# A hybrid encoder block on one core: the weight sums of a seven-product matrix multiply, made by loads, an accumulating DMA and VectorE instead of GpSimd

## The chip, the cores and the metric

The kernel runs on one core of a Trainium2 chip. The metric is the device time of one execution in microseconds. The engines are named as the profile names them: PE is TensorE (PEld its weight loads), DVE is VectorE, ACT is ScalarE, POOL is GpSimd, and SP is the engine whose queue carries most transfers.

## The reference, cut to what matters

The program is one encoder layer on 512 rows of 1024 values: three gated token mixers, an output projection, and a feed-forward block. The change lies in the feed-forward block:

```
x = x + merged @ w_out
h2 = rms_norm(x, g_ffn)                                  # 512 x 1024
ffn = (silu(h2 @ w_ffn_gate) * (h2 @ w_ffn_up)) @ w_ffn_down   # hidden width 2816
return rms_norm(x + ffn, g_final)
```

All values are float32.

## The kernel before, in words

**Precision.** Each float32 operand of a matrix product is split in two reduced parts, `hi` and `lo` (`split`, L85 on ACT makes hi by a copy, L86 on DVE makes lo by a subtraction; L88 and L89 do the same with a scale). A product is three matmuls a step: hi by hi (L104), hi by lo (L105) and lo by hi (L106). The profile cuts a tile's name at its last number, so the tiles `s34_hi`, `a22_lo` and `s12` of the code are `s_hi`, `a_lo` and `s` in its rows, `h2t3h` is the high part of t3, and `po` and `pg` are banks of PSUM.

**The feed-forward block.** The hidden width of 2816 is 22 tiles f of 128. Tiles 0 to 2 are made plainly (`ffn_plain`). Tiles 3 to 21 treat gate and up weights of one tile together as a 2 by 2 matrix of blocks: a holds the gate weights (a11 and a12, its two halves of 512), b the up weights (a21 and a22). With `h2` cut in four blocks they are done in seven block products instead of eight (`ffn_first`, `ffn_second`, `ffn_third`), in the manner of Strassen and Winograd. That takes four sums of weight blocks per tile (s1 to s4, in `lhs_side`) and four sums of blocks of h2, made once (t1 to t4, in `rhs_sums`). A product of a tile is 12 matmuls of 256 columns (4 blocks of 128 rows, three matmuls each), so seven products are 84.

**Loads and buffers.** SP's queue loads a into `raw` (two buffers, shared with all other weight loads) and b into `rawb` (two). POOL makes the four sums into `s12` (two buffers) and `s34r` (one). ACT and DVE split a, s12, s34r and half of b; the split of a and s12 goes to `w_hi` and `w_lo` (three buffers in turn).

**After the products.** ACT and DVE make the gated activation u of a tile. For f from 4 on it is stored to DRAM (L950, SP's queue) and loaded again (L1039) for the last product with `w_ffn_down` (`projection`, called a second time), because the tiles of that product lie where those of the seven products lay.

**Order.** A scheduler puts the instructions of each engine in an order when the program is built; on the chip each engine and each queue then works in that order. A tile's buffer is taken again when those that read it are done.

Of the kernel before, what the change touches and what calls it, by code (L numbers as in the profile page):

```python
# [11 lines left out]
F32 = mybir.dt.float32  # L12
# [3 lines left out]
ALU = mybir.AluOpType  # L16
# [3 lines left out]
P = 128  # L20
S = 512
# [39 lines left out]
def block_kernel(ctx, tc, x, mem, pos, inv, g_mix, mem_g, g_ffn, g_final, g_q, g_kv, gate_bias,  # L61
# [78 lines left out]

    def lhs_side(pool, srcs):
# [33 lines left out]
    with ExitStack() as mix:  # L175
# [684 lines left out]
        gfin_b = keep.tile([P, D], F32, name="gfin_b")  # L860
        bcast_rows(gfin_b, g_final)
# [30 lines left out]
        def projection(banks, w, nch, tail, lhs, hold, early, done, prep=None):  # L892
            vs = []
            for half in range(2):
# [11 lines left out]
                if half == 0:  # L906
                    for t in range(NT):
                        ss = keep.tile([P, 1], F32, name="ssx", tag="ssx", bufs=2 * NT)
                        add_part(parts[t][0][0], t, 0, H, ss)
                        vs.append(partial(ss, EPS))  # L910
                        early(t)
                else:
                    wcs = hold(lead)
                    for t in range(NT):
                        for part in parts[t]:
# [4 lines left out]
                            add_part(ps[:, :n], t, H + c0, n, ss)  # L920
# [14 lines left out]
        projection(((po,) * 4, (po,) * 3, (po, pg)), w_out, 4, 4, lambda c: (mg_hi, mg_lo, 2 * c), hold_out, lambda t: None, to_h2)  # L935
# [42 lines left out]
    def kept(src, name):  # L978
        t = fg.tile([P, HS], F32, name=name, tag=name, bufs=1)
# [3 lines left out]
    def ffn_first(f):  # L983
# [5 lines left out]
        g1 = fg.tile([P, HS], F32, name="g1", tag="g1", bufs=1)  # L989
# [54 lines left out]
    xg = [last.tile([P, D], F32, name=f"xg{t}") for t in range(NT)]  # L1044

# [6 lines left out]
    def store(t, r):  # L1052
# [4 lines left out]
        for c0 in range(H, D, n):  # L1057
# [5 lines left out]
               w_fd, NF // 2, 3, act_side, hold_down, gain_low, store, act_load)  # L1063
# [81 lines left out]
```

## Time and profile before

| | |
|---|---|
| median of 3 runs | 952.23 us (950.2 to 952.91) |
| the profiled execution: its time | 951.96 us |
| its span on the core | 949.0 us |
| busy: PE, DVE, ACT, POOL | 911.5, 649.7, 510.0, 213.7 us |
| tiles by seven products, even part of the stretch | 632.85 to 797.6 us |

The span is the time from the first to the last recorded instruction of the core; the execution's time holds the start and the end around it too. Busy time of an engine is the sum of its instructions; matmuls are pipelined, so a busy PE need not be at its peak. A wait is put down to what came last before the instruction started.

### The profile page before, as it was taken

What the parts mean: (1) busy time and instruction counts of PE and PEld (TensorE: products, weight loads), DVE (VectorE), ACT (ScalarE), POOL (GpSimd) and SP (SyncE); (2) the same over time, 40 slices, a digit from 0 to 9 for tenths busy, and PEclk for the clock granted to TensorE, in tenths of its full rate; (3) what the DMA queues carried; (4) which work ended last, traced back from release to release, by engine and by line L of the source; (5) the groups of instructions that cost most, each with busy time, mean ns of one, the idle gap of its engine ahead of it and who ended that gap; (6) DMA issues with size and microseconds to landing.
All of it is one profiled execution on the core that took longest, in us unless ns stands there. A gap on an engine that the chain in (4) does not pass through costs nothing.

```text
span 949.0 us, 14065 instructions
## 1 busy us (share of the span) xinstructions
PE 911.5 (96%) x5282; PEld 789.7 (83%) x5282; DVE 649.7 (68%) x1031; ACT 510.0 (54%) x896; POOL 213.7 (23%) x215
## 2 busy tenths in 40 slices
PE   7998999999999999999999999989999999799996
PEld 5987887788788788888888789889999999688885
DVE  5678968787766656775557568889888897362322
ACT  7566767776653556777663446444454454251222
POOL 2000002212112101010014100866656652000200
PEclk9999999999999999999999999999999999999999
DMA  7421244444322122112224521323333332382322
GB/s 268 155 73 52 90 138 134 137 134 139 130 93 92 42 89 70 62 51 83 89 79 166 176 69 59 142 99 120 127 112 112 114 134 79 128 268 89 102 76 89
DMA packets 37252, 105.88 MB, mean 112 GB/s; under 512 B 5233, under 2 KB 7601, under 8 KB 37185
## 3 DMA queue, kind: packets, MB, share of 16 engines
q1 hardware_dynamic: 35136, 100.69, 31.8%
q0 software_dynamic: 1184, 3.24, 1.0%
q10 hardware_dynamic: 864, 1.06, 0.3%
q8 instruction: 41, 0.67, 0.3%
q14 instruction: 27, 0.21, 0.1%
HBM read 98.08 MB, written 6.90 MB: 111 GB/s over the span
## 4 chain that ended last, share of the span: by engine, by line
PE 76%; DVE 8%; ACT 4%; DMA 4%; POOL 3%; issue 3%; POOLq 0%; SPq 0%; DVEq 0%; ACTq 0%
PE pg L104 15%; PE pg L105 15%; PE pg L106 15%; PE po L106 5%; PE po L104 5%; PE po L105 5%; DVE s_lo L86 3%; ACT s_hi L85 2%; PE psc L104 2%; PE psc L105 2%; PE psc L106 2%; PE ptp L815 1%; DMA e<-a_dr 1%; DVE w_lo L86 1%; DMA raw<-w_out_d 1%
## 5 line engine op out<-in xcount | busy, mean ns | idle before, releaser
L86 DVE TENSOR_TENSOR w_lo<-raw,w_hi 128x1024 fp32r<-128x1024 f32 (+3 forms) x131 | 151.1, 1155 | 108.8 <-ACT w_hi L85 106.1
L85 ACT ACTIVATE w_hi<-raw 128x1024 fp32r<-128x1024 f32 (+3 forms) x131 | 127.1, 972 | 142.8 <-PE pg L105 86.6
L104 PE MATMUL pg<-h_hi,w_hi 128*128 128x512 f32 (+1 forms) x476 | 175.2, 369 | 1.0 <-DVE q_lo L89 0.6
L105 PE MATMUL pg<-h_lo,w_hi 128*128 128x512 f32 (+1 forms) x476 | 175.6, 369 | 0.0
L106 PE MATMUL pg<-h_hi,w_lo 128*128 128x512 f32 (+1 forms) x476 | 175.1, 368 | 0.3 <-DVE w_lo L86 0.3
L104 PEld LDWEIGHTS pg<-h_hi,w_hi 128*128 128x128 f32 x476 | 89.6, 188 | 15.6 <-DVE q_lo L89 0.8
L106 PEld LDWEIGHTS pg<-h_hi,w_lo 128*128 128x128 f32 x476 | 89.4, 188 | 14.9 <-DVE w_lo L86 0.7
L105 PEld LDWEIGHTS pg<-h_lo,w_hi 128*128 128x128 f32 x476 | 89.5, 188 | 13.6
L571 POOL TENSOR_SCALAR_AFFINE_SELECT e<-e 128x128 f32<-128x128 f32 x64 | 24.6, 394 | 120.3 <-ACT e L568 112.9
L568 ACT ACTIVATE e<-e,ccol 128x512 f32<-128x512 f32 (+3 forms) x64 | 32.3, 554 | 28.7 <-DMA e<-a_dr 28.7
L85 ACT ACTIVATE s_hi<-s34r 128x1024 fp32r<-128x1024 f32 x19 | 20.2, 1061 | 51.3 <-PE pg L105 39.7
L150 POOL TENSOR_TENSOR s<-rawb 128x512 f32<-128x512 f32 x19 | 33.5, 1761 | 62.9 <-DMA rawb<-w_fu_d 62.9
L1070 DVE TENSOR_REDUCE nm<-psc 128x1 f32<-128x512 f32 (+1 forms) x48 | 27.7, 596 | 19.9 <-PE psc L106 19.5
L573 DVE TENSOR_TENSOR e<-e,psc 128x512 f32<-128x512 f32 (+3 forms) x64 | 29.1, 482 | 17.1 <-POOL e L571 15.5
L1073 ACT ACTIVATE pn<-psc,nm 128x512 f32<-128x512 f32 (+1 forms) x48 | 29.3, 613 | 17.7 <-DVE nm L1070 17.6
L86 DVE TENSOR_TENSOR s_lo<-s34r,s_hi 128x1024 fp32r<-128x1024 f32 x19 | 23.4, 1233 | 19.3 <-ACT s_hi L85 19.3
L104 PE MATMUL po<-w_hi,act_hi 128*128 128x512 f32 (+1 forms) x84 | 32.5, 387 | 3.4 <-ACT act_hi L88 3.4
L240 POOL TENSOR_TENSOR merged<-merged,th 128x512 f32<-128x512 f32 x8 | 11.8, 1476 | 104.5 <-DVE th L239 64.7
L86 DVE TENSOR_TENSOR w_lo<-s,w_hi 128x1024 fp32r<-128x1024 f32 x19 | 34.0, 1792 | 1.7 <-ACT w_hi L85 1.7
L153 POOL TENSOR_TENSOR s34r<-raw,s 128x512 f32<-128x512 f32 x19 | 34.7, 1826 | 0.0
L104 PE MATMUL po<-h_hi,w_hi 128*128 128x256 f32 (+1 forms) x116 | 33.7, 291 | 0.9 <-ACT w_hi L85 0.9
L106 PE MATMUL po<-h2t3h,s_lo 128*128 128x256 f32 x76 | 23.3, 306 | 11.8 <-DVE s_lo L86 11.8
(509 smaller groups left out, 2666.9 us busy)
## 6 DMA issues: line engine op xcount, KB each, us to landing
raw<-w_zt_d SPq DMA_DIRECT2D x46, 512.0 KB, 3.4
raw<-w_fg_d SPq DMA_DIRECT2D x22, 512.0 KB, 3.5
raw<-w_fd_d SPq DMA_DIRECT2D x22, 512.0 KB, 3.5
e<-a_dr SPq DMA_DIRECT2D x32, 320.0 KB, 3.5
rawb<-w_fu_d SPq DMA_DIRECT2D x19, 512.0 KB, 3.4
raw<-w_br_d SPq DMA_DIRECT2D x12, 512.0 KB, 3.4
act_dr<-u SPq DMA_DIRECT2D x18, 256.0 KB, 2.6
act<-act_dr SPq DMA_DIRECT2D x18, 256.0 KB, 3.9
```

The costliest lines, as they stand in the source:

```text
L85: A.activation(hi, src, AF.Copy)
L86: V.tensor_tensor(out=lo, in0=src, in1=hi, op=ALU.subtract)
L104: mm(ps, wh, ah, start=start and i == 0, stop=False, skip_group_check=more)
L105: mm(ps, wh, al, start=False, stop=False, skip_group_check=more)
L106: mm(ps, wl, ah, start=False, stop=stop and i == n - 1, skip_group_check=more)
L150: G(out=s12[:, u], in0=b[:, u], in1=b[:, v], op=ALU.add)
L153: G(out=s34[:, v], in0=a[:, v], in1=s12[:, v], op=ALU.subtract)
L568: A.activation(e[:, c0:c0 + n], e[:, c0:c0 + n], AF.Exp, bias=ccol[:, j, d, row:row + 1])
L571: nc.gpsimd.affine_select(out=dg, in_=dg, pattern=[[sgn, P]], compare_op=ALU.is_ge, fill=0.0, base=0, channel_multiplier=-sgn)
L573: V.tensor_tensor(out=e[:, c0:c0 + n], in0=e[:, c0:c0 + n], in1=sc[:, t0:t0 + n], op=ALU.mult)
L1070: nc.vector.tensor_reduce(out=nm, in_=sc, axis=AX.X, op=ALU.max, negate=True)
L1073: nc.scalar.activation(pn, sc, AF.Exp, bias=nm, accum_out=sm)
```

## The change

The sums are chosen so that all are plain additions, up to signs that are taken back elsewhere. s1 and s3 lie in one tile, s13: SP loads a22 into its first half and a11 into its second, and one DMA on POOL's queue, with the addition done by the DMA, adds a21 to both. s2 and s4 lie in s24 and are made by DVE from s13 and a: s2 is s1 + a11, s4 is s2 + a12. s13 and s24 have two buffers each. The tiles m1, g1, u2 and u4 have two instead of one. In `rhs_sums` the signs follow (two sums are now a negated sum in one three-operand instruction), and the activation of tiles from 3 on gets its sign back by a scale of -0.5. Room is found by moving tiles to other pools: the junk tile, the final gain `gfin_b` (whose load then comes later), and rt3; the reloaded `act` tiles move to a pool that exists before the seven products begin.

```diff
@@ rhs_sums
+        def put_neg(name, out, in0, in1):
+            V.scalar_tensor_tensor(out=out, in0=in0, scalar=-1.0, in1=in1, op0=ALU.mult, op1=ALU.subtract)
+            split(*dst[name], out)
+
         put("t3", pool.tile([P, KH, HS], F32, name="rt3"), b22, b12)
-        put("t1", b12, b12, b11)
-        put("t2", b22, b22, b12)
-        put("t4", b21, b21, b22)
+        put("t1", b12, b11, b12)
+        put_neg("t2", b22, b12, b22)
+        put_neg("t4", b21, b22, b21)
@@ lhs_side
-        for raw, src in zip((a, b), srcs):
-            nc.sync.dma_start(out=raw, in_=src)
+        s13, s24 = (pool.tile([P, 1024], F32, name=n, tag=n, bufs=2) for n in ("s13", "s24"))
         u, v = slice(0, 512), slice(512, 1024)
-        s12, s34 = (pool.tile([P, 1024], F32, name=n, tag=n, bufs=b) for n, b in (("s12", 2), ("s34r", 1)))
-        G = nc.gpsimd.tensor_tensor
-        G(out=s12[:, u], in0=b[:, u], in1=b[:, v], op=ALU.add)
-        G(out=s12[:, v], in0=s12[:, u], in1=a[:, u], op=ALU.subtract)
-        G(out=s34[:, u], in0=a[:, u], in1=b[:, u], op=ALU.subtract)
-        G(out=s34[:, v], in0=a[:, v], in1=s12[:, v], op=ALU.subtract)
+        sa, sb = srcs
+        nc.sync.dma_start(out=s13[:, u], in_=sb[:, v])
+        nc.sync.dma_start(out=s13[:, v], in_=sa[:, u])
+        nc.gpsimd.dma_start(out=s13.rearrange("p (i c) -> p i c", i=2),
+                            in_=sb[:, u].unsqueeze(1).to_broadcast([P, 2, 512]), accum_op=ALU.add)
+        nc.sync.dma_start(out=a, in_=sa)
+        nc.sync.dma_start(out=b, in_=sb)
+        V.tensor_tensor(out=s24[:, u], in0=s13[:, u], in1=a[:, u], op=ALU.add)
+        V.tensor_tensor(out=s24[:, v], in0=s24[:, u], in1=a[:, v], op=ALU.add)
...
-        w = both(s12)
-        m |= {"s1": (w, 0), "s2": (w, 512)}
-        w = both(s34, tag="s34")
-        m |= {"s3": (w, 0), "s4": (w, 512)}
+        w = both(s13)
+        m |= {"s1": (w, 0), "s3": (w, 512)}
+        w = both(s24, tag="s24")
+        m |= {"s2": (w, 0), "s4": (w, 512)}
@@ kept, ffn_first
-        t = fg.tile([P, HS], F32, name=name, tag=name, bufs=1)
+        t = fg.tile([P, HS], F32, name=name, tag=name, bufs=2)
...
-        g1 = fg.tile([P, HS], F32, name="g1", tag="g1", bufs=1)
+        g1 = fg.tile([P, HS], F32, name="g1", tag="g1", bufs=2)
@@ act_load
-                a = fin.tile([P, S], F32, name="act", tag="act", bufs=4)
+                a = acte.tile([P, S], F32, name="act", tag="act", bufs=4)
                 nc.sync.dma_start(out=a, in_=act_dr[f - EARLY])
-                split(act_hi[:, f - EARLY], act_lo[:, f - EARLY], a, scale=0.5)
+                split(act_hi[:, f - EARLY], act_lo[:, f - EARLY], a, scale=-0.5)
@@ the last product
+    gfin_b = last.tile([P, D], F32, name="gfin_b")
+    bcast_rows(gfin_b, g_final)
```

What the scheduler makes of it is seen in the even part of the stretch. First DVE, one period, where the tile f = 19 is split. Before (raw_8293 and s12_8297 are f = 19, u_8221 is the activation of f = 18):

```order
L86 TENSOR_TENSOR w_lo_8304<-raw_8293,w_hi_8303 128x1024
L990 TENSOR_TENSOR g1_8216<-po_8189,m1_8214 128x256
L86 TENSOR_TENSOR w_lo_8308<-s12_8297,w_hi_8307 128x1024
L1006 TENSOR_TENSOR u_8221<-po_8133,u4_8160 128x256
L993 SCALAR_TENSOR_TENSOR th_8218<-th_8218,g1_8216 128x256
L86 TENSOR_TENSOR s34_lo_8312<-s34r_8298,s34_hi_8311 128x1024
L1010 SCALAR_TENSOR_TENSOR th_8087<-th_8087,pg_8057 128x256
L1011 TENSOR_TENSOR u_8221<-po_8133,u2_8146 128x256
L86 TENSOR_TENSOR a22_lo_8316<-rawb_8294,a22_hi_8315 128x512
L1012 TENSOR_TENSOR u_8221<-th_8087,u_8221 128x512
```

The same of the changed kernel, one period in which f = 18 is split (raw_8175, s13_8177, s24_8178 are f = 18; s13_8309 and s24_8310 are f = 19). Its source lines are 4 to 6 higher; L158 and L159 are the two sums of s24:

```order
L86 TENSOR_TENSOR w_lo_8187<-raw_8175,w_hi_8186 128x1024
L158 TENSOR_TENSOR s24_8310<-s13_8309,raw_8307 128x512
L1010 TENSOR_TENSOR u_8103<-po_8014,u4_8041 128x256
L86 TENSOR_TENSOR w_lo_8191<-s13_8177,w_hi_8190 128x1024
L994 TENSOR_TENSOR g1_8098<-po_8071,m1_8096 128x256
L159 TENSOR_TENSOR s24_8310<-s24_8310,raw_8307 128x512
L86 TENSOR_TENSOR s24_lo_8195<-s24_8178,s24_hi_8194 128x1024
L1014 SCALAR_TENSOR_TENSOR th_7968<-th_7968,pg_7938 128x256
L997 SCALAR_TENSOR_TENSOR th_8100<-th_8100,g1_8098 128x256
L1015 TENSOR_TENSOR u_8103<-po_8014,u2_8027 128x256
L86 TENSOR_TENSOR a22_lo_8199<-rawb_8176,a22_hi_8198 128x512
L1016 TENSOR_TENSOR u_8103<-th_7968,u_8103 128x512
```

The two sums of f = 19 have come in, the first of them two rows ahead of the split of s13 of f = 18 (w_lo_8191).

Second, SP's queue at the same place. Before, f = 19 and f = 20:

```order
L146 DMA raw_8293<-w_fg_d 128x1024
L146 DMA rawb_8294<-w_fu_d 128x1024
L950 DMA act_dr_5906<-u_7959 128x512
L146 DMA raw_8424<-w_fg_d 128x1024
L146 DMA rawb_8425<-w_fu_d 128x1024
```

Of the changed kernel, f = 19 alone:

```order
L156 DMA raw_8307<-w_fg_d 128x1024
L152 DMA s13_8309<-w_fu_d 128x512
L153 DMA s13_8309<-w_fg_d 128x512
L157 DMA rawb_8308<-w_fu_d 128x1024
L954 DMA act_dr_5904<-u_7971 128x512
```

The two loads of s13 stand between the load of a and that of b.

Third, POOL. Before, f = 19 and f = 20:

```order
L150 TENSOR_TENSOR s12_8297<-rawb_8294 128x512
L151 TENSOR_TENSOR s12_8297<-s12_8297,raw_8293 128x512
L152 TENSOR_TENSOR s34r_8298<-raw_8293,rawb_8294 128x512
L153 TENSOR_TENSOR s34r_8298<-raw_8293,s12_8297 128x512
L150 TENSOR_TENSOR s12_8428<-rawb_8425 128x512
L151 TENSOR_TENSOR s12_8428<-s12_8428,raw_8424 128x512
L152 TENSOR_TENSOR s34r_8429<-raw_8424,rawb_8425 128x512
L153 TENSOR_TENSOR s34r_8429<-raw_8424,s12_8428 128x512
```

Of the changed kernel, from f = 18 to the end of the stretch:

```order
L154 DMA s13_8177<-w_fu_d 128x2x512
L154 DMA s13_8309<-w_fu_d 128x2x512
L154 DMA s13_8441<-w_fu_d 128x2x512
L154 DMA s13_8573<-w_fu_d 128x2x512
L81 DMA gfin_b_8756<-g_final_d 128x1024
```

Four sums a tile have become one DMA a tile, and the load of gfin_b, which stood ahead of the output projection, stands behind the last of them.

## Rows read from the trace of the kernel before

**Rows 1.** The page, part 1: busy time, share of the span, instructions.

```profile
PE 911.5 (96%) x5282; PEld 789.7 (83%) x5282; DVE 649.7 (68%) x1031; ACT 510.0 (54%) x896; POOL 213.7 (23%) x215
```

**Rows 2.** Chain that ended last, 640 to 800 us: start, length, engine, tile, line.

```profile
643.81 1.07 ACT s_hi L85
...
797.58 1.07 ACT s_hi L85
```

**Rows 3.** Windows: length, busy PE, PEld, DVE, ACT, POOL; granted clock, DMA share, GB/s.

```profile
632.85:797.60 164.75, 154.58 (x1262) 151.54 (x1262) 142.64 (x151) 79.92 (x136) 94.61 (x58) 1.00 0.35 117
```

**Rows 4.** Waits, 632.85 to 797.6 us: who for whom, total us, times, longest.

```profile
PEld po L106 <- DVE s_lo L86: 13.2, 15, 0.9
```

**Rows 5.** Timeline within one period: start, length, engine, line, operation, tiles, idle before.

```profile
721.78 1.23 DVE L86 TENSOR_TENSOR s_lo<-s34r,s_hi 128x1024 fp32r<-128x1024 f32 x1 [1.63 <-ACT s_hi L85]
...
722.93 0.41 DVE L1010 SCALAR_TENSOR_TENSOR th<-th,pg 128x256 f32<-128x256 f32 x1
723.06 0.19 PEld L106 LDWEIGHTS po<-h2t3h,s_lo 128*128 128x128 f32 x1 [0.88 <-DVE s_lo L86]
...
723.59 1.33 DVE L86 TENSOR_TENSOR a_lo<-rawb,a_hi 128x512 fp32r<-128x512 f32 x1
...
724.36 0.28 PE L104 MATMUL pg<-h_hi,w_hi 128*128 128x256 f32 x1
...
724.96 0.33 SPq L146 DMA_DIRECT2D rawb<-w_fu_d  x1
...
727.23 0.28 PE L104 MATMUL po<-h_hi,w_hi 128*128 128x256 f32 x1
...
728.43 1.29 POOL L150 TENSOR_TENSOR s<-rawb 128x512 f32<-128x512 f32 x1 [2.35 <-DMA rawb<-w_fu_d]
```

**Rows 6.** Groups by form, 632.85 to 797.6; last row, one tile's: min/median/max ns.

```profile
L86 DVE TENSOR_TENSOR w_lo<-s,w_hi 128x1024 fp32r<-128x1024 f32 x15 | 26.9, 1792 | 0.0
...
L151 POOL TENSOR_TENSOR s<-s,raw 128x512 f32<-128x512 f32 x14 | 25.4, 1812 | 1.1
...
L86 DVE TENSOR_TENSOR a_lo<-rawb,a_hi 128x512 fp32r<-128x512 f32 x15 | 20.1, 1338 | 0.0
...
L86 DVE TENSOR_TENSOR w_lo<-raw,w_hi 128x1024 fp32r<-128x1024 f32 x15 | 18.4, 1226 | 5.8 <-ACT w_hi L85 5.8
...
L993 DVE SCALAR_TENSOR_TENSOR th<-th,g 128x256 f32<-128x256 f32 x16 | 18.0, 1128 | 0.0
...
L86 DVE TENSOR_TENSOR a_lo<-rawb,a_hi x19: 684/1334/1778, 595.0 to 800.5; 128x512 fp32r<-128x512 f32 x19
```

**Rows 7.** DMA issues, whole span: queue, count, KB each, median us to landing.

```profile
rawb<-w_fu_d SPq DMA_DIRECT2D x19, 512.0 KB, 3.4
...
x<-x_d POOLq DMA_DIRECT2D x4, 512.0 KB, 7.9
...
raw<-w_uv_d SPq DMA_DIRECT2D x2, 256.0 KB, 2.6
gfin_b<-g_final_d POOLq DMA_DIRECT2D x1, 512.0 KB, 4.8
gff_b<-g_ffn_d POOLq DMA_DIRECT2D x1, 512.0 KB, 5.2
```

**Rows 8.** Waits of PE from 797.6 us on, and the chain at that place.

```profile
PE po L104 <- ACT act_hi L88: 3.4, 1, 3.4
...
823.91 1.97 DMA act_dr<-u
826.02 2.75 DMA act<-act_dr
828.88 0.64 ACT act_hi L88
```

**Rows 9.** Readers of gfin_b on POOL, and right-hand sums on DVE: min/median/max ns.

```profile
L1050 POOL TENSOR_TENSOR xg<-x,gfin_b x4: 1298/1304/2291, 878.0 to 881.8; 128x512 f32<-128x512 f32 x4
...
L133 DVE TENSOR_TENSOR h_raw<-h_raw x3: 1215/1216/1226, 578.6 to 584.2; 128x1024 f32<-128x1024 f32 x3
```

More of the change, by code (lines that the diff above doesn't have):

```diff
@@ L859, in block_kernel @@
         bcast_rows(gff_b, g_ffn)
-        gfin_b = keep.tile([P, D], F32, name="gfin_b")
-        bcast_rows(gfin_b, g_final)
         x2 = [keep.tile([P, D], F32, name=f"x2_{t}") for t in range(NT)]
@@ L872, in out_mm, with add_part @@
                              w[1][:, k * H + c0:k * H + c0 + n]) for k in range(2)], start=start, stop=stop)
-        def add_part(ps, t, c0, n, ss):
+        def add_part(ps, t, c0, n, ss, pool):
             xs = x2[t][:, c0:c0 + n]
             V.tensor_tensor(out=xs, in0=ps, in1=xs, op=ALU.add)
-            junk = keep.tile([P, H], F32, name="junk", tag="junk", bufs=2)[:, :n]
+            junk = pool.tile([P, H], F32, name="junk", tag="junk", bufs=2)[:, :n]
             A.activation(junk, xs, AF.Square, accum_out=ss)
@@ L890, in partial, with projection @@
             return v
-        def projection(banks, w, nch, tail, lhs, hold, early, done, prep=None):
+        def projection(banks, w, nch, tail, lhs, hold, early, done, pool, prep=None):
             vs = []
@@ L908, in projection @@
                         ss = keep.tile([P, 1], F32, name="ssx", tag="ssx", bufs=2 * NT)
-                        add_part(parts[t][0][0], t, 0, H, ss)
+                        add_part(parts[t][0][0], t, 0, H, ss, pool)
                         vs.append(partial(ss, EPS))
@@ L919, in projection @@
                             ss = keep.tile([P, 1], F32, name="ssx", tag="ssx", bufs=2 * NT)
-                            add_part(ps[:, :n], t, H + c0, n, ss)
+                            add_part(ps[:, :n], t, H + c0, n, ss, pool)
                             if c0 + n < H:
@@ L933, in to_h2 @@
             transpose_split(pt, xn, KD, h2_hi, h2_lo, t, h2_raw)
[L935 removed]
+        projection(((po,) * 4, (po,) * 3, (po, pg)), w_out, 4, 4, lambda c: (mg_hi, mg_lo, 2 * c), hold_out, lambda t: None, to_h2, hx)
     acte = ctx.enter_context(tc.tile_pool(name="acte", bufs=1))
@@ L947, in keep_act @@
         if f < EARLY:
-            split(early[0][:, f], early[1][:, f], u, scale=0.5)
+            split(early[0][:, f], early[1][:, f], u, scale=0.5 if f < PLAIN else -0.5)
         else:
@@ L973, in block_kernel @@
         if f == 0:
-            rhs_sums(ht, h2, h2_raw)
+            rhs_sums(hx, h2, h2_raw)
     hx.release()
@@ L1062, in block_kernel @@
     projection(((po,) * 4, (pg, pg, pt), (pt, po)),
-               w_fd, NF // 2, 3, act_side, hold_down, gain_low, store, act_load)
+               w_fd, NF // 2, 3, act_side, hold_down, gain_low, store, last, act_load)
     for pool in (last, pt, po, pg):
```

## The prediction

> **What bounds the kernel now.** I read the page first: PE is busy 96% of the span, so only work taken from PE, or a wait of PE that goes, can shorten the kernel, and anything that makes PE wait lengthens it [rows 1]. Next the chain that ended last, in the stretch in which the feed-forward tiles f run by seven products. There the reader sees the split of the s34 tile (ACT s_hi, with DVE s_lo behind it) come back every 10.98 us: from 643.81 to 797.58 are 14 steps [rows 2]. Then the stretch itself: 164.75 us are 15 periods, in which DVE is busy 142.64 us (9.51 a period) and POOL 94.61 (6.31) [rows 3]. The waits of that stretch say what PE waits for: s_lo alone, 15 times, 13.2 us on the weight load, 0.88 us a period [rows 4]. The timeline of one period shows it: DVE starts s_lo at 721.78, ends it at 723.01, and the first s_lo weight load goes at 723.06 after 0.88 us of idling [rows 5]. The rest of the period is PE's own pace: 24 products' matmuls of 256 columns from 724.36 to 727.23 give 0.1196 us each, and the 84 of a period 10.04 us. So PE could do a period in 10.04; it takes 10.98. A gain has its ceiling there: 15 periods of 0.94 us are 14 us.
>
> **What is removed.** POOL's four sums, 1.3 to 1.8 us each, leave [rows 5, 6]. With them goes what they did to DVE: the same 128x1024 subtraction takes 1226 ns from raw and 1792 ns from the s tile, the 128x512 one 1338 ns on average and 684 ns at best, the 128x256 gating 1128 ns at L993, while L1010's of that shape takes 0.41 us [rows 5, 6]. DVE's period without the stretching is 3 x 1.23 + 2 x 0.68 + 5 x 0.41 = 7.1 us.
>
> **What is added on DVE.** Two 128x512 sums at 0.68 us, the best of that shape, make 8.5 us. That is less than 9.51 and than PE's 10.04, so the sums themselves cost nothing; PE's matmuls cover them. The second s24 buffer lets the split of s24 start without waiting for the one before, so the s_lo stall could go. The second m1, g1, u2 and u4 buffers free ACT of waits that PE does not wait for: its only wait of the stretch is s_lo [rows 4]. So far the sum would be -14 us.
>
> **What is added on the queues, and the ring it makes.** This decides. Two buffers hold s13. In the order of the changed kernel the loads for f = 19 (s13_8309) must wait until DVE has split f = 17 out of the same buffer (w_lo_8059<-s13_8045). Then come, each after the one before has landed: two SP loads, POOL's accumulating DMA, and DVE's first s24 sum of f = 19. That sum stands in DVE's order two rows ahead of the split of f = 18 (w_lo_8191<-s13_8177), and that split frees the buffer for f = 20. DVE runs in order, so from one split of s13 to the next the whole chain lies on the path once per tile, whatever PE does. Queued behind the waiting sum are the u sum, the split of s13, g1, the second s24 sum and the s24 split: PE's products with S1, S2 and S3 all wait with it.
>
> Its length, step by step. DVE's end to SP's issue: a_lo ends at 724.92, SP issues at 724.96, 0.04 us [rows 5]. Two loads of 256 KB: one of that size lands after 2.6 us, one of 512 KB after 3.4 [rows 7]; the two share the engines, so 3.4 (2.95 if the second, issued 0.33 us later, were not slowed). Landing to the waiting engine: 724.96 + 3.4 = 728.36, POOL starts at 728.43, so 0.07, and the same again for DVE. The first s24 sum 0.68, the u sum 0.41, the split 1.23, less 0.08 twice, by which DVE's neighbours overlap in the timeline (721.78 + 1.23 against 722.93). Without the accumulating DMA that is 5.75 us.
>
> No row shows an accumulating DMA. The nearest are the plain 512 KB DMAs on POOL's queue: 4.8, 5.2 and 7.9 us from issue to landing, the last for four issued together [rows 7]. An accumulate must read its destination besides its source. One more pass over 512 KB is 1.6 us: 256 KB more cost 0.8 on SP's queue (2.6 against 3.4, rows 7). I take 5.2, since the gff_b load, like these, ran by itself on its queue beside SP's loads, plus 1.6: **6.8 us**. Below: 4.8, if the second read hides wholly. Above: 5.2 + 2 x 1.6 = 8.4, if the write-back costs a pass too or the 512 KB load of b, issued some 3 us after these, takes its share; 7.9 + 1.6 = 9.5 with both.
>
> The Trainium skill's page "DMA: Bandwidth & Descriptors", section "Anatomy of one DMA", gives a fit for a DMA of this queue, 2.0 us plus the bytes at 436 GB/s, which makes 3.2 us for 512 KB. The trace has 4.8 and 5.2 for that size [rows 7], so I go by the rows; with 3.2 the ring would be 8.95 us, under PE's 10.04, and the kernel would gain as in the second rival below.
>
> So the ring is 5.75 + 6.8 = 12.55 us against 10.98, +1.57 a tile. In the new order every tile from f = 6 to f = 21 has its first s24 sum ahead of the split before it, but for f = 8; 15 steps make +23.6 us.
>
> **Where the stretch ends.** PE waits 3.4 us for act_hi after the last u, which the chain shows as a store of 1.97 us and a reload of 2.75 [rows 8]. The act buffers move to a pool that exists earlier, and the order has four act loads among the loads of f = 9 to 12, so the first down chunks need no load behind the last store. The split of act_hi (0.64 us there) still follows: I take -3 us, bounds 0 and -3.4. Those four loads stand ahead of s13's loads in SP's queue and wait for their own stores; the sums before them on DVE cover that, since the split that frees s13 ends some 2.8 us after the u that is stored (two splits of 1.23 and a u sum).
>
> **What costs nothing.** The gain gfin_b is loaded on POOL after the last accumulate; its first reader starts at 878.0 [rows 9], tens of us later. If it came late POOL alone would wait. The two negated right-hand sums are three-operand instructions on the same elements as the 1.2 us ones before [rows 9]; 0 to 0.5 us. Signs and the pools of junk and rt3 move nothing in time.
>
> **Sum.** The profiled execution took 951.96 us, its span 949.0; the median of the runs, 952.23, is 0.3 above it. 952 + 23.6 - 3 = 972.6, say **973 us**. As a rule for any length a of the accumulate: 949 + 15 x (a - 5.23) us, down to a = 4.29, where PE's 10.04 takes over.
>
> **Rivals.**
> - *The accumulate is nearly as short as a plain DMA* (the other side). At the 4.8 us of gfin_b [rows 7] the ring is 10.55, and the time 949 - 6.5 = 943. It decides at a = 5.4, where the two cancel. For it: the 4.8 itself, and that DMA engines were only 35% busy [rows 3]. Against: the second read has to hide, and SP adds 512 KB a tile.
> - *POOL's DMA is as quick as SP's.* With 3.4 us for 512 KB [rows 7] the ring fits under PE's work, the s_lo stall goes, and the time is 949 - 14 = 935. Against it: every 512 KB row on that queue is at least 4.8. The Trainium skill's fit, above, points here.
> - *The accumulate is much longer*: 8.4 gives 997, 9.5 gives 1013. For it: twice the descriptors (256 rows of 2 KB against 128 of 4 KB), and more traffic around each transfer than gff_b had.
> - *DVE becomes the bound* by its two sums: 8.5 us against 10.04, so it would have to run 18% slower than its best. I count it as part of the first two cases: it costs nothing there.
>
> **How the numbers follow.** A run of this kernel can be told from no change at about 0.3%, 3 us: a below 5.2 is faster, above 5.6 slower. Chances: a from 5.6 to 8.4, my forecast, 0.57 (954 to 997, its own range); longer 0.17; from 5.2 to 5.6, no change, 0.07; shorter, but ring-bound, 0.13; PE-bound 0.06. So slower 0.74, same 0.07, faster 0.19. The range from 940 to 1003 holds a from 4.6 to 8.8; outside are PE's floor and the far end of the long case, about 0.19.
>
> **What would show it.** Right: an even step of about 12.5 us between splits of s13; DVE idle 2 us or more a tile ahead of its first s24 sum (L158), waiting for the accumulating DMA; PE idle by about 2.5 us a tile where it had 0.88; accumulates landing after some 6.8 us; no wait for act_hi of 3 us. DVE's subtractions back at 1.23 and 0.68 us. Wrong: accumulates under 5 us, steps of 10.0 to 10.9, and PE at work through the stretch; or PE idle on s24_lo while the accumulate landed long before, which would put the blame on DVE's order and not on the DMA.

## The result, and the profile after

The changed kernel takes 1007.0 us (median of 4 runs, 1001.3 to 1010.0), the kernel before 952.6 (4 runs beside them): a ratio of 1.0568, 95% interval 1.0509 to 1.0627. It is 5.7% slower; the prediction was 973 us, with a range to 1003. The profiled execution took 1004.1 us, its span is 1002.2, 53.2 more than before.

First the page of the changed kernel, part 1:

```profile
PE 929.7 (93%) x5282; PEld 808.7 (81%) x5282; DVE 615.2 (61%) x1069; ACT 507.8 (51%) x896; POOL 107.5 (11%) x158
```

POOL and DVE have both less to do than in [rows 1], and PE has the same 5282 matmuls, so the loss is not in added work; that PE is busy 18.2 us longer goes with the granted clock of the next row. The windows, for the stretch of the seven products (columns as in [rows 3]):

```profile
600.00:860.00 260.00, 207.80 (x1511) 203.02 (x1510) 141.70 (x219) 97.40 (x164) 21.62 (x18) 0.90 0.62 167
```

PE idles 52.2 us of 260. The granted clock fell from 1.00 to 0.90, that is, to its lower level (1.2 GHz) at times. Around one idle time of PE, which lasts from 800.0 to 802.2 us, it was:

```profile
800.50:802.00 1.50, 0.00 (x0) 0.00 (x0) 0.90 (x2) 0.00 (x0) 0.00 (x0) 1.00 0.51 203
803.00:805.00 2.00, 2.00 (x11) 2.00 (x11) 2.00 (x4) 0.98 (x3) 0.00 (x0) 0.50 0.32 91
806.00:813.00 7.00, 7.00 (x60) 7.00 (x60) 2.76 (x4) 3.99 (x6) 1.21 (x1) 1.00 0.73 178
```

After the idle time PE worked at 0.50 for some 3 us, and then at 1.00 again. It idled again from 814.0 us on, and no step of the turn shown below waits for PE, so the slower PE is not what sets the step. How the steps stretched is read from the rows of one instruction, the low part of the first sum tile (s12 before, s13 after): count, ns, and the start of the first and the last. Before:

```profile
L86 DVE TENSOR_TENSOR w_lo<-s,w_hi x19: 1214/1979/2347, 600.4 to 794.4; 128x1024 fp32r<-128x1024 f32 x19
```

and after:

```profile
L86 DVE TENSOR_TENSOR w_lo<-s,w_hi x19: 1212/1217/1225, 607.8 to 854.6; 128x1024 fp32r<-128x1024 f32 x19
```

The 18 steps took 194.0 us and take 246.8: all of the loss, +52.8, lies between the first and the last of these splits. (The first comes 7.4 us later, but what follows the last one is 7.0 shorter.) The split itself went from 1979 to 1217 ns in the middle, since no sum of POOL runs beside it. Now the waits of DVE and PE from 590 to 860 us, and last PE's waits behind 860 (who for what, us in total, times, longest):

```profile
DVE s L158 <- DMA s<-w_fu_d: 86.6, 17, 8.1
...
PE po L104 <- DVE u L1010: 22.8, 8, 5.7
PE po L106 <- DVE w_lo L86: 9.6, 2, 5.2
PE po L104 <- DVE g L994: 8.4, 2, 4.5
PE pg L106 <- DVE s_lo L86: 5.8, 1, 5.8
...
PE po L104 <- ACT act_hi L88: 1.7, 1, 1.7
```

DVE waits 86.6 us for the accumulating DMA, at its first s24 sum (L158). What PE waits for (u, the low part of s13, g1, the low part of s24) are the instructions that stand behind that sum in DVE's order. The wait of [rows 4], for s_lo at the product with t3, is gone; s_lo is now the low part of s24, and PE waits for it once. The wait for act_hi of [rows 8] went from 3.4 to 1.7 us. The DMA issues of the page (KB each, us to landing):

```profile
raw<-w_fg_d SPq DMA_DIRECT2D x22, 512.0 KB, 4.8
...
rawb<-w_fu_d SPq DMA_DIRECT2D x19, 512.0 KB, 4.5
s<-w_fu_d POOLq DMA_DIRECT2D x19, 512.0 KB, 8.2
...
s<-w_fu_d SPq DMA_DIRECT2D x19, 256.0 KB, 2.8
```

The accumulating DMA lands 8.2 us after its issue, and the load of b 4.5 where it was 3.4 [rows 7]. One turn of the ring, from the timeline (columns as in [rows 5]): f = 17 is split from 802.05 on, f = 18 from the end of the piece on, and the loads are those of f = 19.

```profile
802.05 1.22 DVE L86 TENSOR_TENSOR w_lo<-s,w_hi 128x1024 fp32r<-128x1024 f32 x1
...
803.29 0.33 SPq L152 DMA_DIRECT2D s<-w_fu_d  x1
...
803.67 0.43 SPq L153 DMA_DIRECT2D s<-w_fg_d  x1
...
806.96 0.33 SPq L157 DMA_DIRECT2D rawb<-w_fu_d  x1
807.19 1.21 POOL L154 DMA_DIRECT2D s<-w_fu_d  x1 [12.64 <-DVE a_lo L86]
807.56 0.33 SPq L954 DMA_DIRECT2D act_dr<-u  x1
...
810.57 0.33 SPq L156 DMA_DIRECT2D raw<-w_fg_d  x1
815.43 0.69 DVE L158 TENSOR_TENSOR s<-s,raw 128x512 f32<-128x512 f32 x1 [4.89 <-DMA s<-w_fu_d]
816.04 0.42 DVE L1010 TENSOR_TENSOR u<-po,u 128x256 f32<-128x256 f32 x1
816.37 1.22 DVE L86 TENSOR_TENSOR w_lo<-s,w_hi 128x1024 fp32r<-128x1024 f32 x1
```

Split to split is 14.32 us (802.05 to 816.37): 1.24 to SP's first issue, 3.90 to POOL's issue, 8.24 to the s24 sum, 0.94 to the next split. Each step is there as foretold, and each waits for the one before. The name behind POOL's idle time is an earlier event: what its DMA needs last by the program is the s13 loads, and the second of them landed 3.0 us after its issue, at 806.7. Three more transfers start from 0.2 us before the accumulate's issue to 3.4 us after it: b, the store of u, and the next a.

### The profile page after: what moved, and what is told of

The parts are those of the page before. It is cut to its first block, busy times and chain, and to the rows that moved or that the text cites. A ratio compares the mean times of both kernels' runs of the same rounds, so it can differ in the third digit from the quotient of the medians.

```text
span 1002.2 us, 14116 instructions
## 1 busy us (share of the span) xinstructions
PE 929.7 (93%) x5282; PEld 808.7 (81%) x5282; DVE 615.2 (61%) x1069; ACT 507.8 (51%) x896; POOL 107.5 (11%) x158
## 4 chain that ended last, share of the span: by engine, by line
PE 66%; DMA 16%; DVE 10%; issue 4%; ACT 2%; POOL 0%; SPq 0%; DVEq 0%; POOLq 0%; ACTq 0%
PE pg L104 12%; PE pg L106 12%; PE pg L105 12%; DMA s<-w_fu_d 10%; PE po L104 4%; PE po L106 4%; PE po L105 4%; DVE w_lo L86 3%; DMA s<-w_fg_d 2%; PE psc L104 2%; PE psc L105 2%; PE psc L106 2%; PE ptp L821 1%; DMA e<-a_dr 1%; DMA raw<-w_fg_d 1%
## 5 line engine op out<-in xcount | busy, mean ns | idle before, releaser
L106 PEld LDWEIGHTS pg<-h_hi,w_lo 128*128 128x128 f32 x476 | 89.7, 188 | 14.7 <-DVE w_lo L86 0.5
L158 DVE TENSOR_TENSOR s<-s,raw 128x512 f32<-128x512 f32 x19 | 13.1, 691 | 86.6 <-DMA s<-w_fu_d 86.6
L154 POOL DMA_DIRECT2D s<-w_fu_d x19 | 22.9, 1204 | 244.2 <-DVE a_lo L86 76.6
L104 PE MATMUL po<-h2t4h,a_hi 128*128 128x256 f32 x76 | 25.2, 331 | 22.8 <-DVE u L1010 22.8
L996 ACT ACTIVATE th<-g 128x256 f32<-128x256 f32 x19 | 7.9, 415 | 71.4 <-DVE g L994 71.4
L106 PE MATMUL po<-h_hi,w_lo 128*128 128x256 f32 (+1 forms) x116 | 34.7, 300 | 9.6 <-DVE w_lo L86 9.6
L104 PEld LDWEIGHTS po<-h2t4h,a_hi 128*128 128x128 f32 x76 | 17.1, 225 | 24.4 <-DVE u L1010 24.4
L577 POOL TENSOR_SCALAR_AFFINE_SELECT e<-e 128x128 f32<-128x128 f32 x64 | 23.5, 375 | 122.8 <-ACT e L574 114.1
L105 PE MATMUL po<-h_lo,w_hi 128*128 128x256 f32 (+1 forms) x116 | 34.4, 296 | 0.0
L104 PE MATMUL po<-h2t3h,w_hi 128*128 128x256 f32 x76 | 25.1, 331 | 9.7 <-DVE g L994 8.4
```

What stands on the lines that cost most here:

```text
L104: mm(ps, wh, ah, start=start and i == 0, stop=False, skip_group_check=more)
L105: mm(ps, wh, al, start=False, stop=False, skip_group_check=more)
L106: mm(ps, wl, ah, start=False, stop=stop and i == n - 1, skip_group_check=more)
L154: nc.gpsimd.dma_start(out=s13.rearrange("p (i c) -> p i c", i=2), in_=sb[:, u].unsqueeze(1).to_broadcast([P, 2, 512]), accum_op=ALU.add)
L158: V.tensor_tensor(out=s24[:, u], in0=s13[:, u], in1=a[:, u], op=ALU.add)
L577: nc.gpsimd.affine_select(out=dg, in_=dg, pattern=[[sgn, P]], compare_op=ALU.is_ge, fill=0.0, base=0, channel_multiplier=-sgn)
```

## The experiments

Each kernel ran beside the kernel before on the same chip; kernels measured at other times ran on other chips, so the ratio says more than the difference of two medians. Kernels 3, 6, 9 and 10 do not make all the sums, and their results are not the program's. The last three columns are of the profiled execution: the median landing of the DMA on POOL's queue over the whole span (for 10 over the stretch from 620 to 840 us, where most of its tiles run; 4.7 us over all 19), the 18 steps from the first to the last split of s13 (s12 in the kernel before), and the span.

| kernel | median, us | ratio (95% interval) | lands, us | 18 steps, us | span |
|---|---|---|---|---|---|
| before | 951.8 to 954.3 | 1 | | 194.0 | 949.0 |
| after | 1007.0 | 1.0568 (1.0509 to 1.0627) | 8.2 | 246.8 | 1002.2 |
| 1, third s13 buffer | 958.4 | 1.0047 (1.0026 to 1.0068) | 8.6 | 199.5 | 954.8 |
| 2, s13 summed on POOL | 939.2 | 0.9856 (0.9836 to 0.9877) | none | 184.8 | 937.2 |
| 3, copy without adding | 974.2 | 1.0224 (1.0194 to 1.0253) | 5.7 | 217.7 | 970.9 |
| 4, before with two s34r | 960.1 | 1.0074 (1.0047 to 1.0101) | none | 201.9 | 957.8 |
| 5, all sums on DVE | 929.7 | 0.9746 (0.972 to 0.9771) | none | 176.9 | 927.4 |
| 6, accumulate in 4 KB rows | 1008.9 | 1.057 (1.0534 to 1.0606) | 7.5 | 253.4 | 1008.6 |
| 7, one s24 buffer | 957.9 | 1.0036 (1.0013 to 1.006) | 9.6 | 203.4 | 958.6 |
| 8, traffic beside kernel 5 | 968.6 | 1.0144 (1.0107 to 1.018) | 7.8 | 215.0 | 965.4 |
| 9, three buffers, no adding | 934.8 | 0.9812 (0.9789 to 0.9836) | 6.0 | 176.7 | 933.2 |
| 10, half accumulated | 980.2 | 1.0288 (1.0264 to 1.0312) | 4.2 | 224.9 | 980.0 |
| 11, kernel 5, one buffer each | 933.5 | 0.9802 (0.9784 to 0.982) | none | 177.7 | 929.8 |
| 12, traffic beside kernel 11 | 931.2 | 0.9766 (0.9737 to 0.9794) | 9.0 | 178.1 | 928.4 |

One reading goes through the table: the span without the 18 steps is 750 to 757 us in every kernel, 755 in the one before. What sets the time of each kernel is the step of a tile, and nothing else of the change costs more than 2 us.

**1. A third buffer for s13.** The ring then goes over two tiles.

```diff
-        s13, s24 = (pool.tile([P, 1024], F32, name=n, tag=n, bufs=2) for n in ("s13", "s24"))
+        s13, s24 = (pool.tile([P, 1024], F32, name=n, tag=n, bufs=k) for n, k in (("s13", 3), ("s24", 2)))
```

> The changed kernel with three s13 buffers instead of two. If the ring is only the wait for a free s13 buffer, a third buffer gives the chain two tiles of time, PE sets the pace at about 10.0 us a tile, and the time is 935 to 945 us. If it is DVE's order that ties the accumulating DMA to the next split (in this build the scheduler uses the third buffer to set the first s24 sum still further ahead), DVE still waits for each accumulate and the time stays at 985 to 1010 us.

It gave back 48.6 of the 54.4 us, and not the rest: neither expectation held. The DMA part of the stretch from 620 to 800 us shows why:

```profile
s<-w_fu_d POOLq DMA_DIRECT2D x15, 512.0 KB, 8.6
raw<-w_fg_d SPq DMA_DIRECT2D x15, 512.0 KB, 7.1
...
s<-w_fu_d SPq DMA_DIRECT2D x14, 256.0 KB, 6.5
```

With transfers of two tiles under way at once, every landing is longer: the loads of s13 6.5 us where they took 2.8. Over the tiles from f = 9 on, the timeline gives a ring of 23.5 us for two tiles, 11.75 a tile. That is still above PE's 10.04. DVE waits at L158 for two things in about equal parts, from 590 to 860 us: 27.5 us for the accumulate and 26.1 us for the load of a. Whether it is the traffic that costs, or the wait for it, was left to runs 8, 9 and 12.

**2. s13 by two POOL sums,** with no load and no accumulate for it; s24 stays on DVE.

```diff
-        nc.sync.dma_start(out=s13[:, u], in_=sb[:, v])
-        nc.sync.dma_start(out=s13[:, v], in_=sa[:, u])
-        nc.gpsimd.dma_start(out=s13..., accum_op=ALU.add)
+        nc.gpsimd.tensor_tensor(out=s13[:, u], in0=b[:, u], in1=b[:, v], op=ALU.add)
+        nc.gpsimd.tensor_tensor(out=s13[:, v], in0=b[:, u], in1=a[:, u], op=ALU.add)
```

> The changed kernel with s13 made by two POOL sums from a and b (its two loads and the accumulating DMA are gone); s24 still by two DVE sums, second buffers kept. If the accumulating DMA is what costs, the ring goes and the time is 915 to 935 us, PE idle under 10 us in the stretch. If DVE's two added sums, or the new order, cost, it stays above 960 us. If only POOL's stretching of DVE's instructions had mattered before, it is near 950.

The loss turns into a gain of 1.4%; the time, 939.2, is just outside the 915 to 935 us that were expected. From 620 to 800 us PE is busy 174.26 us of 180, so it still waits some 0.3 us a tile, and none of that is for s_lo. All that the queues' chain took is gone when the transfers go.

**3. The same DMA without the addition.**

```diff
-                            in_=sb[:, u].unsqueeze(1).to_broadcast([P, 2, 512]), accum_op=ALU.add)
+                            in_=sb[:, u].unsqueeze(1).to_broadcast([P, 2, 512]))
```

> The changed kernel with the DMA on POOL's queue as a plain copy (it does not add, so s1 and s3 are a21 alone). If the addition (second read, doubled time of a packet) makes the DMA long, it lands after some 5.5 us instead of 8.2 and the time is 950 to 970 us. If it is POOL's making of the descriptors for rows of 2 KB, it lands after 7 to 8 us and the time stays at 985 to 1005 us.

From the page's DMA issues:

```profile
s<-w_fu_d POOLq DMA_DIRECT2D x19, 512.0 KB, 5.7
```

The same shape on the same queue lands in 5.7 us: so the addition costs 2.5 of the 8.2 us. The time falls by 32.8 us, to 4 us above what was expected, and the kernel is still 2.2% slower than before: the ring costs even with a plain DMA in it.

**4. The kernel before with two s34r buffers,** to see whether the single buffer made the s_lo stall of [rows 4].

```diff
-... for n, b in (("s12", 2), ("s34r", 1)))
+... for n, b in (("s12", 2), ("s34r", 2)))
```

> The kernel before with a second s34r buffer and nothing else. If the single buffer made the 0.88 us stall of s_lo, the stall goes and the time is 935 to 943 us. If DVE's lengthened instructions made it, the stall stays, though it may wait elsewhere, and the time is 950 to 953 us.

PE's wait from 620 to 800 us, in the kernel before and in this one:

```profile
PE po L106 <- DVE s_lo L86: 11.8, 17, 0.9
```

```profile
PE po L106 <- DVE s_lo L86: 18.9, 15, 1.3
```

The stall grew, and the kernel became 0.7% slower. So the single buffer was not its cause, against my account of it; the time is above both expected ranges, though the second reason, lengthened instructions, is what the trace shows. The split for which PE waits, before and here (min/median/max ns), with what POOL waited for before between the two:

```profile
L86 DVE TENSOR_TENSOR s_lo<-s34r,s_hi x17: 1225/1225/1377, 621.6 to 798.7; 128x1024 fp32r<-128x1024 f32 x17
```

```profile
POOL s34r L152 <- DVE s_lo L86: 31.4, 16, 2.4
```

```profile
L86 DVE TENSOR_TENSOR s_lo<-s34r,s_hi x16: 1531/1852/1853, 624.2 to 798.0; 128x1024 fp32r<-128x1024 f32 x16
```

With one buffer POOL had to wait until DVE had made s_lo, so no sum of POOL ran beside that split. With two, POOL's sums run beside it (L151 to 729.11 us and L153 from 729.19 on, beside a split from 728.34 to 730.19), and the split takes 1.85 us for 1.23. That is 0.6 us a tile, as much as PE's wait grew (from 0.69 to 1.26 us).

**5. All four sums on DVE.**

```diff
-        nc.sync.dma_start(out=s13[:, u], in_=sb[:, v])
-        nc.sync.dma_start(out=s13[:, v], in_=sa[:, u])
-        nc.gpsimd.dma_start(out=s13..., accum_op=ALU.add)
+        V.tensor_tensor(out=s13[:, u], in0=b[:, u], in1=b[:, v], op=ALU.add)
+        V.tensor_tensor(out=s13[:, v], in0=b[:, u], in1=a[:, u], op=ALU.add)
```

> The changed kernel with all four sums on DVE, in 128x512 sums of 0.69 us: no sum on POOL, no load of s13, no accumulating DMA. DVE has 9.8 us of work a tile against PE's 10.04. If the accumulating DMA is what costs, and DVE without POOL beside it keeps its short times, the time is 925 to 940 us, at or under the kernel with two POOL sums (939). If DVE's sums bind, steps are over 11 us and the time is above 955 us.

The window from 620 to 800 us:

```profile
620.00:800.00 180.00, 180.00 (x1479) 178.81 (x1479) 148.73 (x236) 91.40 (x155) 0.00 (x0) 1.00 0.41 129
```

PE never idles, and DVE with four sums a tile has 31 us to spare. This is the fastest of the versions beside its kernel before: 2.5% (interval in the table). It is 7.7% below the changed one by the two medians, 929.7 and 1007.0, which were not measured side by side.

**6. The accumulate in rows of 4 KB** instead of pieces of 2 KB.

```diff
-        nc.gpsimd.dma_start(out=s13.rearrange("p (i c) -> p i c", i=2),
-                            in_=sb[:, u].unsqueeze(1).to_broadcast([P, 2, 512]), accum_op=ALU.add)
+        nc.gpsimd.dma_start(out=s13, in_=sb, accum_op=ALU.add)
```

> The changed kernel with the accumulating DMA in 128 rows of 4 KB (b as it lies is added, so s1 and s3 are not the right sums) instead of 256 rows of 2 KB; the same bytes are added. If half of the 8.2 us hangs on the number of rows (POOL is busy 1.20 us on it against 0.55 for a plain DMA of 128 rows), it lands after 7 us or less and the time is 980 to 995 us. If bytes alone count, it lands after 8 us and the time stays at 1000 to 1010 us.

```profile
s<-w_fu_d POOLq DMA_DIRECT2D x19, 512.0 KB, 7.5
```

That row of the page's DMA issues says that half as many pieces save 0.7 us of 8.2. The time did not fall, because the scheduler put more of DVE's work between the sum and the next split (from the sum's start to the split's end 3.9 us, as the median of the timeline's tiles from f = 9 on; 2.16 in the changed kernel).

**7. One s24 buffer,** which moves DVE's first s24 sum behind the split of the tile before.

```diff
-        s13, s24 = (pool.tile([P, 1024], F32, name=n, tag=n, bufs=2) for n in ("s13", "s24"))
+        s13, s24 = (pool.tile([P, 1024], F32, name=n, tag=n, bufs=k) for n, k in (("s13", 2), ("s24", 1)))
```

DVE's order in this kernel, where s13_8177 is f = 18 and s13_8309 f = 19 as in the order shown with the change:

```
935 L86 TENSOR_TENSOR w_lo_8191<-s13_8177,w_hi_8190 128x1024
...
941 L158 TENSOR_TENSOR s24_8310<-s13_8309,raw_8307 128x512
...
947 L86 TENSOR_TENSOR w_lo_8323<-s13_8309,w_hi_8322 128x1024
```

> The changed kernel with one s24 buffer instead of two: the first s24 sum of a tile then stands in DVE's order six rows behind the split of s13 of the tile before, not two ahead of it, so that split no longer waits for the accumulating DMA. Nothing else changes. If DVE's order makes the ring, the accumulate has two tiles of time and the time falls to 930 to 965 us, although a buffer was taken away. If the length of the DMAs or their traffic binds by itself, it stays at 990 to 1015 us.

The sum of f = 19 now stands six rows behind the split of f = 18, not two ahead of it, so the chain of one tile spans two steps. A buffer less takes 49 us off, about what a buffer more for s13 did. The accumulate landed after 9.6 us there, longer than in any other kernel, and the time still fell: with two s13 buffers it was the order of DVE that made the ring span one tile.

**8. The transfers alone.** The loads and the accumulate of the changed kernel beside kernel 5, into a tile of two buffers that nothing reads (m1, u2 and u4 with one buffer, for room).

```diff
+        dum = pool.tile([P, 1024], F32, name="dum", tag="dum", bufs=2)
+        nc.sync.dma_start(out=dum[:, u], in_=sb[:, v])
+        nc.sync.dma_start(out=dum[:, v], in_=sa[:, u])
+        nc.gpsimd.dma_start(out=dum..., in_=..., accum_op=ALU.add)
```

> All four sums on DVE as in e5_dve_all, and beside them the two loads and the accumulating DMA of every tile into a buffer that nothing reads (two of them; m1, u2 and u4 back to one buffer for room). If the traffic of these transfers slows the weight loads enough to matter by itself, the time is over 15 us above e5_dve_all. If only waiting for the accumulate costs, it is within 5 us of it.

It cost 39 us over kernel 5, but this run does not tell what it was made for. SP's waits show it:

```profile
SPq L155 <- DMA dum<-w_fu_d: 74.2, 17, 9.0
```

The load into the unread tile waited for the accumulate of two tiles before, up to 9.0 us, and held up the loads of a and b behind it on SP's queue: from 620 to 800 us DVE waited 30.4 us for the load of b. Run 12 mends that.

**9. Three s13 buffers, and no adding.** The edits of runs 1 and 3 together.

> Three s13 buffers, and the DMA on POOL's queue copies without adding, so s1 and s3 are a21 alone (the sums are not made). With three buffers a split frees the buffer for the tile after the next but one, so the ring spans two tiles. Theory A, it is the time that the addition costs the DMA engines that holds the kernel with three buffers at 958 us: the plain copy lands in some 6 us, the ring is some 20 us for two tiles, about PE's own 10.04 a tile, and the time is 930 to 945 us. Theory B, the mere extra traffic of a third load, added or not, holds it there: 950 to 960 us.

Its window and DMA rows from 620 to 800 us:

```profile
620.00:800.00 180.00, 176.85 (x1455) 175.07 (x1454) 132.17 (x206) 91.15 (x156) 10.56 (x15) 1.00 0.65 217
```

```profile
s<-w_fu_d POOLq DMA_DIRECT2D x15, 512.0 KB, 6.0
raw<-w_fg_d SPq DMA_DIRECT2D x15, 512.0 KB, 5.8
...
s<-w_fu_d SPq DMA_DIRECT2D x14, 256.0 KB, 5.2
```

Theory A held, in time and in landing: against run 1 all three landings are 1.3 to 2.6 us shorter, and PE is busy all but 3 us. The same loads move (217 GB/s, 204 in run 1), so a third load as such does not hold the kernel back.

**10. Half of the accumulate,** into the first half of s13 alone.

```diff
-        nc.gpsimd.dma_start(out=s13.rearrange("p (i c) -> p i c", i=2),
-                            in_=sb[:, u].unsqueeze(1).to_broadcast([P, 2, 512]), accum_op=ALU.add)
+        nc.gpsimd.dma_start(out=s13[:, u], in_=sb[:, u], accum_op=ALU.add)
```

> The accumulating DMA adds a21 to the first half of s13 alone (128 x 512, 256 KB), so s3 is a11 alone (one sum is not made). Theory A, the landing goes with the bytes: of 8.2 us some 3 are there for any DMA of this queue and 5.2 go with 512 KB, so half of it lands after 5.6 to 6.2 us, the ring is shorter by some 2.3 us a tile, and the time is 960 to 975 us. Theory B, the addition costs a fixed time: it lands after 7.5 us or more, and the time is 990 to 1007 us.

Its DMA row from 620 to 840 us, and DVE's timeline from the sum that waited to the split:

```profile
s<-w_fu_d POOLq DMA_DIRECT2D x16, 256.0 KB, 4.2
```

```profile
793.48 0.69 DVE L157 TENSOR_TENSOR s<-s,raw 128x512 f32<-128x512 f32 x1 [1.95 <-DMA s<-w_fu_d]
794.09 0.68 DVE L1015 TENSOR_TENSOR u<-th,u 128x512 f32<-128x512 f32 x1
794.69 1.22 DVE L86 TENSOR_TENSOR w_lo<-raw,w_hi 128x1024 fp32r<-128x1024 f32 x1
795.82 0.42 DVE L1009 TENSOR_TENSOR u<-po,u 128x256 f32<-128x256 f32 x1
796.16 0.68 DVE L158 TENSOR_TENSOR s<-s,raw 128x512 f32<-128x512 f32 x1
796.76 1.22 DVE L86 TENSOR_TENSOR w_lo<-s,w_hi 128x1024 fp32r<-128x1024 f32 x1
```

The landing about halves with the bytes, from 8.2 to 4.2 us in this stretch (4.7 over all tiles), below theory A's figure, so theory B fell. Theory A's 3 us for any DMA of this queue has no row: the DMAs of 4 to 16 KB on it (`a_dr<-brel`, page of the changed kernel) land after 1.6 to 2.2 us. The kernel still takes 980 us, 5 more than theory A gave, because the u product, the split of a and the second s24 sum have come between: 4.50 us from the sum's start to the split's end here (793.48 to 797.98), 3.9 to 4.5 from f = 9 on, against 2.16. A shorter wait came with a longer queue behind it.

**11. Kernel 5 with one buffer each** for s13, s24, m1, g1, u2 and u4.

> All four sums on DVE as in the kernel of 929.7 us, but with one buffer each for s13, s24, m1, g1, u2 and u4. Theory A, where no transfer is in the ring the second buffers give nothing: PE stays busy through the stretch and the time is 928 to 933 us. Theory B, the second buffers are part of the gain: PE waits again for the low part of a sum, about 0.5 to 0.9 us a tile, and the time is 936 to 945 us.

```profile
620.00:800.00 180.00, 180.00 (x1472) 178.36 (x1470) 149.83 (x235) 91.63 (x154) 0.00 (x0) 1.00 0.42 130
```

The window shows PE at work throughout, and the time is 0.5 us above theory A's bound. Once no transfer stands in the ring the second buffers are worth at most some 0.5% (ratios 0.9746 and 0.9802, taken on different chips).

**12. The transfers alone, with nothing waiting.** Kernel 11 with the unread tile of run 8 in three buffers, each set tied to its place by a copy of one column.

```diff
+        dum = pool.tile([P, 1024], F32, name="dum", tag="dum", bufs=3)
+        if prev:
+            nc.gpsimd.tensor_copy(out=dum[:, 0:1], in_=prev.pop()[:, 0:1])
+        prev.append(b)
```

> All four sums on DVE with one buffer each, as in the kernel of 933.5 us, plus the two s13 loads and the accumulating DMA of each tile into a tile that nothing reads, of three buffers (a one-column copy on POOL ties each set to its place in the order). No work waits for these transfers by its data; what they cost is the DMA engines' time and SP's queue. Theory A, the kernels with three s13 buffers and with one s24 buffer stayed at 958 us because of the transfers' own traffic: loads of a and b land after 5 us and more, DVE waits for them, and the time is 945 to 960 us. Theory B, the traffic costs nothing unless something waits for the sums: PE stays busy through the stretch, 932 to 940 us.

Window and DMA rows from 620 to 800 us:

```profile
620.00:800.00 180.00, 179.76 (x1469) 178.04 (x1469) 151.32 (x238) 92.87 (x156) 23.89 (x29) 1.00 0.82 219
```

```profile
raw<-w_fg_d SPq DMA_DIRECT2D x15, 512.0 KB, 6.9
dum<-w_fu_d POOLq DMA_DIRECT2D x15, 512.0 KB, 9.0
```

This is the run that settles it. The DMA engines are busy 82% of the stretch, more than in any other kernel; accumulates land after 9.0 us and loads of a after 6.9; PE is busy 179.76 of 180 us, and the time is that of kernel 11 or below. So the transfers cost nothing here by their traffic. Their landing times are paid where an engine's next step waits for them, and in the changed kernel that is once per tile. Theory A fell. Run 1 then stays at 958 us because its two-tile ring has to wait for these long landings, and run 9 is quicker because they are shorter; that is read from their rings and landings, not tried by itself.

## Why the prediction was right in kind and short in size

**The ring** was right: its place, its members, its order and the engine that waits. DVE's wait at L158 for the accumulate, PE's waits for what is queued behind it, and steps that PE does not set, are what the text asked for. Runs 2 and 5 (no transfers), 1 (a buffer more) and 7 (another place of the sum) each break the ring in another way and give back 49 to 77 us.

**The step that failed** is the length of the transfers in it, first the term of the accumulate, 5.2 plus 1.6, 6.8 us. It measured 8.2. Run 3 splits that: 5.7 for the plain DMA where I took 5.2, and 2.5 for the addition where I took one pass over the bytes, 1.6. My upper bound, 8.4, was the right value's neighbour. The second term that was short is the loads: I took 3.51 us from the split's end to POOL's issue, by rows of loads that ran nearly alone [rows 7]. From f = 9 on the timeline's tiles have 4.6 on average, 3.9 at f = 19. Run 3 shows this term without the addition: with 5.7 us for the accumulate the prediction's rule gives 956 us, and it took 974; the same stretch is 4.5 us there.

**The sum again, with measured terms.** From f = 9 on, the mean of a turn is 4.60 + 8.16 for the accumulate to the sum + 2.39 from the sum to the next split's end = 15.15, where I had 3.51 + 6.87 + 2.17 = 12.55. Of the 2.6 us missing, the accumulate is 1.3, the loads 1.1 and the rest 0.2. The 15 steps of which the prediction spoke took 225.4 us, 15.03 each, 37 us more than forecast; the exempted step, that of f = 8, took 7.6 us where it had taken 10.98, and gave 3.4 back. The forecast's 20.6 (23.6 less 3), with 37 more and 3.4 less, is 54, against 53.2 in the span.

**The act loads** were perhaps not free. They are issued from 649.3 to 694.3 us, and the three turns of that time (f = 9 to 11) took 17.3 us on average, those of f = 17 to 21 14.3: 9 us of the 37. I had put them under cover of DVE's sums, and thought of their place in the queue, not of what they do to the landing of the loads beside them (7.4 us from the second issue to POOL's at f = 9, 3.4 to 3.7 at f = 17 to 21). But f = 12 took 17.0 us although its act load went out 7.2 us ahead of its s13 loads, and in f = 11 and 12 two more of DVE's instructions stand between the sum and the split (4.0 and 3.9 us instead of 2.16). No run took the act loads away, so how much of it is theirs stays open.

**What else was right.** DVE's added sums cost nothing: the split is back at 1217 ns, and run 5 shows DVE with all four sums unhurried beside a PE that never idles. So "DVE becomes the bound" was never near. The second buffers for m1, g1, u2 and u4 bring little (runs 5 and 11, 929.7 and 933.5, measured beside different runs of before and without the second s13 and s24 too). Of the -3 us at the end of the stretch, 1.7 shows in the wait for act_hi. The ceiling of 14 us for a PE that never waits was about right too: with it 935 us was given for the case without a ring, and runs 11 and 5, in which PE never waits in the stretch, took 933.5 and 929.7.

**What was wrong beside it.** I read the s_lo stall as a matter of s34r's one buffer ("the second s24 buffer lets the split start"). Run 4 denies that: a second buffer does not remove the stall. The trace of the kernel before shows another reason. The first product that reads the split of a tile's s34 is that with t3. In PE's order it comes right behind the products with s4 and a22 of the tile two before (f = 19 behind f = 17), and the split goes into the buffers that this product with s4 has just left:

```profile
720.31 0.28 PE L105 MATMUL pg<-h_lo,s_hi 128*128 128x256 f32 x1
...
720.69 1.06 ACT L85 ACTIVATE s_hi<-s34r 128x1024 fp32r<-128x1024 f32 x1 [2.65 <-PE pg L105]
...
721.99 0.28 PE L104 MATMUL po<-h2t3h,s_hi 128*128 128x256 f32 x1
```

ACT's and DVE's 2.3 us of splitting (720.69 to 723.01, [rows 5]) have only the a22 product to hide under, some 1.4 us. In the changed kernel s3 lies with s1, and the first product that reads the split of s24 is that with t2. In run 11:

```profile
701.10 1.23 DVE L86 TENSOR_TENSOR s_lo<-s,s_hi 128x1024 fp32r<-128x1024 f32 x1 [1.12 <-ACT s_hi L85]
...
705.92 0.28 PE L104 MATMUL pg<-h2t2h,s_hi 128*128 128x256 f32 x1
```

The split is ready 3.6 us ahead. PE has no wait for s_lo in run 2 either, where POOL still makes two sums, so it is not their absence that removes it. That the regrouping of the sums did is read from these traces; no run undoes it alone. (In the order shown with the change, u_8221 is the activation of f = 17, not 18: it goes to the 14th tile of `act_dr`.)

**The rivals.** "The accumulate is much longer" came near: 8.2 us lies just inside my own forecast of 5.6 to 8.4, and by the prediction's rule it gives 994 us; the rest of the way to 1007 is mainly the loads. The two short ones failed: on POOL's queue plain DMAs of 512 KB landed after 5.7 and 6.0 us among these loads (runs 3 and 9), accumulating ones after 7.5 to 9.6, and even at that queue's plain speed the kernel would not have gained (run 3). The fit in the Trainium skill's page "DMA: Bandwidth & Descriptors", section "Anatomy of one DMA", makes an estimate of 3.2 us of 512 KB on this queue. No row here has so short a landing of that size on it, and the measurement decides.

## What to carry to other kernels

Before replacing an engine's work by transfers, follow the buffer back: if a load may start only when an engine has finished with the tile before, and that engine stands in front of the load's result in its own order, then the whole latency of the transfers is on the path once per tile, even with DMA engines that are far from busy (a share of 0.62 here). Price such a latency with the other transfers of the same moment in it, not by a row of one that ran alone; and break the ring by a buffer more, or by moving the waiting instruction behind the one that frees the buffer. An engine that is not the bound may make the sums at no cost to PE: here DVE, idle 31 us of 180 with all four of them.

## What the runs showed of the hardware that was not expected

- An accumulating DMA takes longer than a plain one of its shape and queue: 8.2 against 5.7 us for 128x2x512, and in time on the DMA engines too (POOL's queue took 22.1% of 16 engines from 620 to 840 us for 15 of them, 3.2 us each, against 14.7% of 180 us for 15 plain ones in run 9, 1.8 us each). It went mostly with the bytes (4.2 to 4.7 us for 256 KB) and little with the size of its rows (7.5 us with rows of 4 KB).
- Landing times doubled under load without costing anything: the loads of a, 512 KB, from 3.5 us before to 6.9 us at a DMA share of 0.82 (run 12). The load of b, of the same size, landed after 4.1 us in the same stretch.
- The granted clock went from 1.00 to 0.90 in the stretch where PE idled a fifth of the time, and stood at 1.00 in every kernel whose PE stayed at work (runs 2, 5, 9, 11 and 12). The idle share alone does not order the kernels: from 620 to 800 us run 4 idled 20.2 us at 1.00, with no wait above 1.5 us, and run 1 idled 16.6 us at 0.97, with one of 2.4.
- A second buffer made the kernel before slower by 0.7% (run 4): it let a sum of POOL run beside a split on DVE, which then took 1.85 us for 1.23.
